# A second block that begins with the weights still in place, operand loads on GpSimd's queue, and pinned column sums

## The chip, the core and the metric

The kernel runs on one core of a Trainium2 chip. TensorE multiplies matrices, VectorE (DVE in the profile) and ScalarE (ACT) work on tiles, GpSimd (POOL) computes a few small values and issues some DMAs, and SyncE (SP) only issues DMAs. The metric is the device time of one execution in microseconds (us); lower is better. A difference of 0.2%, about 4.4 us here, is what a measurement of this kernel can tell from no change.

## What is computed

One encoder layer on a sequence of 2048 rows of 1024 columns: a normalisation and an input projection, windowed attention beside a state-space scan, a joint output projection ("the join" below), and then a gated feed-forward part and a last normalisation. The change touches the feed-forward part:

```
h = rms_norm(x, norm_ffn_g)                        # 2048 x 1024
up = depthwise_conv(h @ w_up, conv_w, conv_b)      # w_up: 1024 x 5632, conv of width 3 along the rows
gate, val = up[..., :2816], up[..., 2816:]
x = x + (silu(gate) * val) @ w_down                # w_down: 2816 x 1024
return rms_norm(x, norm_final_g)
```

All of it is float32. The kernel splits every operand into a high part in TensorE's rounded float32 format and a low rest, and adds three products (high by high, high by low, low by high).

## The kernel before

Both feed-forward products go by Strassen's scheme in Winograd's form: a step computes a 2 by 2 block product with seven half-size products instead of eight, from sums and differences of the quarter matrices. TensorE works through steps. The rows are cut into two blocks of 1024 (b = 0, 1), and block b has 22 steps, one for each pair f of a gate tile and a value tile of `w_up`. After these 44 steps (n = 0 to 43) come 24 steps of the down projection in three parts. A step of the up projection has 7 products of 12 matmuls, each matmul 128x128 by 128x512.

**Moving operand** (the rows of the block; seven matrices named in `BOP`: "11", "t2", "21", "t1", "t3", "t4", "22"). `put(b, m)` loads one of them from HBM in two halves of 512 KB through a ring of three buffers (tile `braw`, pool `fr`) and splits each half: ScalarE writes the high part (L1009), VectorE the low part (L1010). They stay for a whole block. The last step of a block calls `put` for the next block after each product. For block one, `ffn_open` loads the first four during the join, and `meet` the last three, after the last turn of the join. All these loads are issued by SyncE (L1007).

**Stationary operand** (the weights of one f). `up_raw` loads the gate tile and the value tile (`uraw`, L1015, 512 KB each). `stationary` splits g (L1048 on ScalarE, L1049 on VectorE), forms the sums s0 and s1 (tiles `st`) and splits s2, g2, s1 and s4 from them. There is one buffer of each split tile, so a split for the next step waits until the products that read the tile are over. In block one the sums are four VectorE operations of 128x512 (L1061 to L1064), and SyncE then stores both to HBM (L1072, L1073). In block two the two sums are loaded (L1058, L1059) instead.

**One step** on TensorE: products 1 and 6 of the step, 4 of the step before, 2, then 3 of the step before, 5 and 7. The PSUM results are joined on VectorE (L1159, L1164, L1175, L1179, L1180) and ScalarE (L1156 copies product 1 to `cu`, L1172); `up_conv` then does the convolution (L1232 to L1243), Silu (L1246) and the gate (L1247), and GpSimd stores the result (L1250).

**Sums of `w_down`.** For the down projection, `down_sums` makes 11 sets of sums: SyncE loads two rows of tiles into the same ring of three buffers (tile `bsum`, L1099), VectorE does four operations of 128x512 (L1101 to L1104), GpSimd stores four results (L1106). A table `SUMS` names the steps that call it: in block one the loads at n = 9, 12, 15, 18 and the operations one step after each, in block two every second step from n = 24.

A scheduler reorders each engine's instructions, so the place in the code is not the place in the queue. It drew the first eleven sums' operations forward: those of block one stand within its first four steps, those of block two within that block's first six steps. `keep_in_program_order` ties an instruction to its place in the program.

`rstd` (L124, L125) computes the scale of a row's normalisation: one VectorE operation and a power on GpSimd, needed by each turn of the join.

## Time and profile before

| | |
|---|---|
| time, median of 3 runs | 2192.28 us (2191.86 to 2192.76) |
| the profiled execution's own time | 2187.94 us |
| its span, first to last instruction | 2186.1 us |
| mean granted TensorE clock | 0.980 |
| TensorE busy | 2074.6 us (95%) |
| VectorE busy | 1692.2 us (77%) |
| ScalarE busy | 1047.1 us (48%) |
| GpSimd busy | 142.7 us (7%) |
| first product of step 0 (block one) | 852.77 us |
| first product of step 22 (block two) | 1284.24 us |

Busy time is a share of the whole span. How well a stage feeds TensorE is seen in the stretches: the number of matmuls that start in one, and the idle time ahead of an instruction with the engine that ended it.

### The profile page before, as it was taken

The page shows a single profiled execution, that of the slowest core. Times are in us where ns is not written, and L with a number is a line of the kernel's source. Part 1 is how long each engine was busy: PE and PEld are TensorE (multiplying, and loading weights), DVE is VectorE, ACT ScalarE, POOL GpSimd, SP SyncE. Part 2 cuts the span into 40 slices and gives each one's busy share as a digit, 9 for nine tenths or more (in the row PEclk, how much of TensorE's full clock was granted, in tenths as well). Part 3 has the DMA queues.
Part 4 walks back from the last instruction along what each step waited for, and adds up shares of the span by engine and source line. Part 5 has one row for each costly group of instructions (what it writes and reads, how often), then busy time and mean ns, then how long its engine had stood idle before and what let it go on. Part 6 is the DMA issues. An engine that isn't in the chain of part 4 may idle for free.

```text
span 2186.1 us, 28134 instructions
## 1 busy us (share of the span) xinstructions
PE 2074.6 (95%) x10000; PEld 1668.5 (76%) x10000; DVE 1692.2 (77%) x2977; ACT 1047.1 (48%) x1836; POOL 142.7 (7%) x230
## 2 busy tenths in 40 slices
PE   7998988799999998999999999999999999999997
PEld 5787777577777776788888877788888777787886
DVE  8978888675566557898888888877777987867875
ACT  5524444776666654444444464444444623324332
POOL 0400000000000000100000001100000000000111
PEclk9999999899999999999999999999999999999999
DMA  7965665523243229763334377743444667756542
GB/s 278 340 187 152 198 185 163 161 95 90 83 130 116 82 93 293 266 230 137 133 145 145 135 240 261 264 143 129 141 135 133 200 226 248 239 159 230 193 158 93
DMA packets 221612, 384.12 MB, mean 176 GB/s; under 512 B 15264, under 2 KB 136608, under 8 KB 221472
## 3 DMA queue, kind: packets, MB, share of 16 engines
q1 hardware_dynamic: 201744, 316.72, 45.5%
q0 software_dynamic: 16288, 62.92, 7.6%
q10 hardware_dynamic: 3440, 2.69, 0.4%
q8 instruction: 78, 1.28, 0.2%
q14 instruction: 62, 0.51, 0.1%
HBM read 254.88 MB, written 127.40 MB: 175 GB/s over the span
## 4 chain that ended last, share of the span: by engine, by line
PE 53%; issue 23%; DVE 10%; DMA 8%; ACT 3%; POOL 2%; SPq 1%; ACTq 0%; POOLq 0%; DVEq 0%
PE py L1132 13%; PE px L1132 8%; PE pz L1132 8%; PE po L78 3%; PE po L79 3%; PE po L80 3%; PE av L591 2%; PE ptp L581 2%; PE sp L558 2%; DMA kp_d<-kk 1%; PE pp L80 1%; PE pp L79 1%; PE pp L78 1%; PE gpt L669 1%; DMA m<-kp_d 1%
## 5 line engine op out<-in xcount | busy, mean ns | idle before, releaser
L1132 PE MATMUL px<-b,g1h 128*128 128x512 f32 x1056 | 328.0, 391 | 13.4 <-ACT cu L1156 13.4
L1132 PEld LDWEIGHTS px<-b,g1h 128*128 128x128 f32 x1056 | 199.4, 189 | 56.2 <-ACT cu L1156 14.6
L1132 PE MATMUL px<-b,g1l 128*128 128x512 f32 x528 | 206.8, 392 | 3.5 <-DVE g1l L1049 3.5
L1132 PE MATMUL py<-bt,g2h 128*128 128x512 f32 x528 | 168.9, 397 | 7.9 <-DVE cu L1179 7.9
L1132 PE MATMUL py<-bt,s2h 128*128 128x512 f32 x528 | 165.8, 395 | 10.1 <-ACT s2h L1048 10.1
L1132 PE MATMUL pz<-bt,s1h 128*128 128x512 f32 x528 | 163.7, 391 | 4.8 <-ACT s1h L1048 4.8
L1132 PE MATMUL pz<-b,s4h 128*128 128x512 f32 x528 | 162.8, 389 | 0.0
L1132 PE MATMUL py<-bt,s1h 128*128 128x512 f32 x528 | 162.6, 389 | 0.0
L1132 PEld LDWEIGHTS py<-bt,s2h 128*128 128x128 f32 x528 | 99.2, 189 | 33.6 <-ACT s2h L1048 13.7
L1132 PEld LDWEIGHTS py<-bt,g2h 128*128 128x128 f32 x528 | 100.8, 192 | 31.1 <-issue 5.4
L1132 PEld LDWEIGHTS px<-b,g1l 128*128 128x128 f32 x528 | 100.0, 189 | 25.3 <-DVE g1l L1049 4.4
L1132 PEld LDWEIGHTS pz<-bt,s1h 128*128 128x128 f32 x528 | 99.2, 188 | 26.3 <-ACT s1h L1048 5.9
L1132 PEld LDWEIGHTS pz<-b,s4h 128*128 128x128 f32 x528 | 99.1, 188 | 20.6
L1132 PEld LDWEIGHTS py<-bt,s1h 128*128 128x128 f32 x528 | 99.1, 188 | 20.6
L1048 ACT ACTIVATE g2h<-uraw 128x512 fp32r<-128x512 f32 x44 | 27.9, 634 | 176.7 <-PE py L1132 176.7
L1048 ACT ACTIVATE s1h<-st 128x1024 fp32r<-128x1024 f32 (+1 forms) x68 | 70.1, 1031 | 85.3 <-PE py L1132 78.0
L1132 PE MATMUL py<-bt,s2l 128*128 128x512 f32 x264 | 105.6, 400 | 3.1 <-DVE s2l L1049 3.1
L1164 DVE TENSOR_TENSOR cu<-py,cu 128x512 f32<-128x512 f32 x68 | 46.9, 690 | 74.6 <-PE py L1132 74.6
L1132 PE MATMUL py<-bt,g2l 128*128 128x512 f32 x264 | 104.4, 395 | 0.0
L1132 PE MATMUL pz<-bt,s1l 128*128 128x512 f32 x264 | 102.7, 389 | 0.0
L1132 PE MATMUL py<-bt,s1l 128*128 128x512 f32 x264 | 102.7, 389 | 0.0
L1132 PE MATMUL pz<-b,s4l 128*128 128x512 f32 x264 | 102.7, 389 | 0.0
(280 smaller groups left out, 5094.5 us busy)
## 6 DMA issues: line engine op xcount, KB each, us to landing
uraw<-in_w_up_dram SPq DMA_DIRECT2D x88, 512.0 KB
us<-st SPq DMA_DIRECT2D x44, 512.0 KB
st<-us SPq DMA_DIRECT2D x44, 512.0 KB
araw<-act SPq DMA_DIRECT2D x32, 512.0 KB
xr<-sum SPq DMA_DIRECT2D x32, 512.0 KB
xr<-in_xT_dram SPq DMA_DIRECT2D x30, 512.0 KB
act<-cv POOLq DMA_DIRECT2D x22, 512.5 KB, 3.1
bsum<-in_w_down_dram SPq DMA_DIRECT2D x22, 512.0 KB
```

What stands on the lines that cost most here:

```text
L78: nc.tensor.matmul(out, sh, mh, start=first and i == 0, stop=False)
L79: nc.tensor.matmul(out, sh, ml, start=False, stop=False)
L80: nc.tensor.matmul(out, sl, mh, start=False, stop=last and i == n - 1)
L558: nc.tensor.matmul(sp[:, :n], qTs[b][:, 4 * kv + j], kT[:, kv, i, slots], start=i == 0, stop=i == 1)
L581: nc.tensor.transpose(pt[:, 128 * j:128 * (j + 1)], sm[:, j, 128 * ki:128 * ki + 128], self.ident)
L591: nc.tensor.matmul(av[64 * o:64 * o + 64], vt[order[ki]][:, kv], ph4[:, o], start=ki == 0, stop=ki == len(order) - 1)
L669: nc.tensor.transpose(pt[:, 128 * k:128 * (k + 1)], src[:, 128 * k:128 * (k + 1)], self.ident)
L1048: S.activation(h[:, :c], src, AF.Copy)
L1132: nc.tensor.matmul(bank, x[:, k], o[:, y, k], start=first and k == 0 and i == 0, stop=k == kn - 1 and i == 2, skip_group_check=True)
L1164: V.tensor_tensor(old["vc"][:, lo], old["Y"], old["vc"][:, lo], op=ALU.add)
```

## The change

Five edits. (1) Block two goes through f = 21, 0, 1, ..., 20 instead of 0 to 21, and its first step (n = 22) takes the split weights that step 21 left in place; nothing is loaded or split for it. (2) The sums s0 and s1 are neither stored nor loaded: block two computes them with the same four VectorE operations as block one. (3) The 14 loads of the moving operand for block one are issued by GpSimd instead of SyncE. (4) The `put` calls for the last three moving operands of block one stand in step 0 behind the copy of product 1 (L1156 before) instead of in `meet`, ahead of it. (5) The four operations of `down_sums` are pinned to their places in the program. Line numbers of the changed kernel are lower by one around L1009, by five to eight from `stationary` on.

```diff
--- before.py
+++ after.py
@@ -105,7 +105,6 @@
         self.bop_d = [{m: d.tile([128, 4, HALF], F32, name=f"bo{b}{m}") for m in BOP} for b in (0, 1)]
         self.act_d = [d.tile([2 * n, 128, L], F32, name=f"act{c}") for c, n in enumerate(DN)]
         self.wsum_d = [{m: d.tile([128, n, HALF], F32, name=f"ws{c}{m}") for m in ("t1", "t2", "t3", "t4")} for c, n in enumerate(DN)]
-        self.usum_d = [d.tile([2, 128, 8, 128], F32, name=f"us{f}") for f in range(NF)]
         self.gN = None
         self.st_f = ExitStack()
         self.left = False
@@ -976,7 +975,7 @@
         self.operands(self.pool(st, "fb"), BOP[:2])
         self.pw = self.pool(st, "fu")
         yield
-        self.w0 = yield from self.up_weights(0, 0, self.pw)
+        self.w0 = yield from self.up_weights(0, self.pw)
         for n in BOP[:2]:
             yield from self.put(0, n)
         while not self.left:
@@ -1004,7 +1003,7 @@
                 r, c = int(n[0]) - 1, int(n[1]) - 1
                 f = DF[b - 2] + r * kn + k
                 src = self.a["w_down"][128 * f:128 * (f + m), HALF * c:HALF * (c + 1)].rearrange("(k p) c -> p k c", p=128)
-            nc.sync.dma_start(raw, src)
+            (nc.sync if b else nc.gpsimd).dma_start(raw, src)
             h = o[:, 0, k:k + m]
             nc.scalar.activation(h, raw, AF.Copy)
             nc.vector.tensor_tensor(o[:, 1, k:k + m], raw, h.bitcast(F32), op=ALU.subtract)
@@ -1031,13 +1030,9 @@
         self.sv = p.tile([128, 2 * NF, 2], F32, name="sv", bufs=1)
         pz = self.pool(st, "fpz", 2, space=PSUM)
         self.psq = self.pool(st, "fpq", space=PSUM)
-        for n in BOP[4:]:
-            for _ in self.put(0, n):
-                pass
         return p, pz
 
-    def stationary(self, g, v, n, pw, sums=None, keep=False):
-
+    def stationary(self, g, v, n, pw):
 
         nc = self.nc
         V, S = nc.vector, nc.scalar
@@ -1054,29 +1049,22 @@
         s0 = pw.tile([128, 8, 128], F32, tag="st0", name=self.nm("st0"))
         s1 = pw.tile([128, 8, 128], F32, tag="st1", name=self.nm("st1"))
         yield
-        if sums is not None and not keep:
-            nc.sync.dma_start(s1, sums[1])
-            nc.sync.dma_start(s0, sums[0])
-        else:
-            V.tensor_tensor(s0[:, lo], v[:, lo], v[:, hi], op=ALU.add)
-            V.tensor_tensor(s1[:, lo], s0[:, lo], g[:, lo], op=ALU.subtract)
-            V.tensor_tensor(s0[:, hi], g[:, lo], v[:, lo], op=ALU.subtract)
-            V.tensor_tensor(s1[:, hi], g[:, hi], s1[:, lo], op=ALU.subtract)
-            yield
+        V.tensor_tensor(s0[:, lo], v[:, lo], v[:, hi], op=ALU.add)
+        V.tensor_tensor(s1[:, lo], s0[:, lo], g[:, lo], op=ALU.subtract)
+        V.tensor_tensor(s0[:, hi], g[:, lo], v[:, lo], op=ALU.subtract)
+        V.tensor_tensor(s1[:, hi], g[:, hi], s1[:, lo], op=ALU.subtract)
+        yield
         s2, = split("s2", s1[:, lo], 4)
         a22, = split("g2", v[:, hi], 4)
         yield
         s1_, s3 = split("s1", s0[:, 0:2 * n], 8)
         s4, = split("s4", s1[:, hi], 4)
-        if keep:
-            nc.sync.dma_start(sums[1], s1)
-            nc.sync.dma_start(sums[0], s0)
         yield
         return {1: (a11, "11"), 2: (a12, "21"), 3: (s4, "22"), 4: (a22, "t4"), 5: (s1_, "t1"), 6: (s2, "t2"), 7: (s3, "t3")}
 
-    def up_weights(self, b, f, pw):
+    def up_weights(self, f, pw):
         g, v = (self.up_raw(f, i) for i in (0, 1))
-        return (yield from self.stationary(g, v, 4, pw, self.usum_d[f], b == 0))
+        return (yield from self.stationary(g, v, 4, pw))
 
     def down_rows(self, c, t, pw):
 
@@ -1098,10 +1086,10 @@
             for t, f in ((A, f0 + k), (B, f0 + n + k)):
                 nc.sync.dma_start(t.rearrange("p n c -> p (n c)"), self.a["w_down"][128 * f:128 * (f + 1), :])
             yield
-            V.tensor_tensor(C[:, 0], A[:, 1], A[:, 0], op=ALU.subtract)
-            V.tensor_tensor(C[:, 1], B[:, 1], A[:, 1], op=ALU.subtract)
-            V.tensor_tensor(A[:, 0], C[:, 1], A[:, 0], op=ALU.add)
-            V.tensor_tensor(B[:, 0], B[:, 0], A[:, 0], op=ALU.subtract)
+
+            for o, x, y, op in ((C[:, 0], A[:, 1], A[:, 0], ALU.subtract), (C[:, 1], B[:, 1], A[:, 1], ALU.subtract),
+                                (A[:, 0], C[:, 1], A[:, 0], ALU.add), (B[:, 0], B[:, 0], A[:, 0], ALU.subtract)):
+                self.tc.keep_in_program_order(V.tensor_tensor(o, x, y, op=op))
             for m, t in (("t1", C[:, 0]), ("t3", C[:, 1]), ("t2", A[:, 0]), ("t4", B[:, 0])):
                 nc.gpsimd.dma_start(self.wsum_d[c][m][:, k], t)
             yield
@@ -1113,7 +1101,8 @@
         V, S = nc.vector, nc.scalar
         lo, hi = slice(0, HALF), slice(HALF, BLK)
 
-        todo = [(b, f, f == NF - 1) for b in (0, 1) for f in range(NF)]
+
+        todo = [(0, f, f == NF - 1) for f in range(NF)] + [(1, (f - 1) % NF, f == NF - 1) for f in range(NF)]
         todo += [(2 + c, t, t == NB - 2) for c in range(3) for t in range(0, NB, 2)]
 
         def run(steps):
@@ -1140,7 +1129,10 @@
             if at:
                 b, f, _ = at
                 down = b >= 2
-                w = self.w0 if n == 0 else run(self.down_rows(b - 2, f, self.pw) if down else self.up_weights(b, f, self.pw))
+                if n == 0:
+                    w = self.w0
+                elif n != NF:
+                    w = run(self.down_rows(b - 2, f, self.pw) if down else self.up_weights(f, self.pw))
                 X, Y = (ps.tile([128, HALF], F32, tag=t, name=self.nm(t)) for t in ("px", "py"))
                 cur = {"w": w, "at": at, "Y": Y}
                 if n == 0:
@@ -1157,6 +1149,9 @@
                 if n:
                     product(cur, 6, Y, True)
                 V.tensor_tensor(gc[:, hi], Y, vc[:, hi], op=ALU.add)
+                if n == 0:
+                    for m in BOP[4:]:
+                        run(self.put(0, m))
                 if down:
                     V.tensor_tensor(gc[:, hi], gc[:, hi], xg[:, hi], op=ALU.add)
             if old:
```

ScalarE's queue at the end of the join, before: `hT` is the join's last turn, `bt_1888`, `bt_1889` and `b_1890` are "t3", "t4" and "22", and `cu_9050` is the copy of product 1 of step 0.

```order
L739 ACTIVATE hT_8986<-gpt_8981 128x512
L750 ACTIVATE hT_8996<-gpt_8990 128x512
L1009 ACTIVATE bt_1888_9011<-braw_9024 128x1024
L1009 ACTIVATE bt_1888_9011<-braw_9028 128x1024
L1009 ACTIVATE bt_1889_9012<-braw_9032 128x1024
L1156 ACTIVATE cu_9050<-px_8952 128x512
L1009 ACTIVATE bt_1889_9012<-braw_9036 128x1024
L1048 ACTIVATE g1h_9096<-uraw_9092 128x1024
L1009 ACTIVATE b_1890_9013<-braw_9040 128x1024
L1009 ACTIVATE b_1890_9013<-braw_9044 128x1024
```

ScalarE's queue at the same place, after:

```order
L738 ACTIVATE hT_8962<-gpt_8957 128x512
L749 ACTIVATE hT_8972<-gpt_8966 128x512
L1148 ACTIVATE cu_9002<-px_8928 128x512
L1008 ACTIVATE bt_1888_8987<-braw_9005 128x1024
L1008 ACTIVATE bt_1888_8987<-braw_9009 128x1024
L1008 ACTIVATE bt_1889_8988<-braw_9013 128x1024
L1043 ACTIVATE g1h_9072<-uraw_9068 128x1024
L1167 ACTIVATE cg_9001<-px_8928 128x512
L1043 ACTIVATE s1h_9090<-st_1904_9076 128x1024
L1008 ACTIVATE bt_1889_8988<-braw_9017 128x1024
```

The copy of product 1 (`cu`) moves from behind three splits of "t3" and "t4" to ahead of all of them.

GpSimd's queue there, after; the rows at L124 are the power operations of the join's normalisations, and before only these stood there:

```order
L1006 DMA braw_8848<-bo_112 128x1024
L124 TENSOR_TENSOR r_1820_8637<-rsv_8638,mhalf 128x1
L1006 DMA braw_8871<-bo_112 128x1024
L124 TENSOR_TENSOR ra_8667<-rsv_8668,mhalf 128x1
L1006 DMA braw_8895<-bo0t_113 128x1024
L124 TENSOR_TENSOR r_1860_8805<-rsv_8806,mhalf 128x1
L1006 DMA braw_8905<-bo0t_113 128x1024
L1006 DMA braw_9005<-bo0t_114 128x1024
L1006 DMA braw_9009<-bo0t_114 128x1024
L1006 DMA braw_9013<-bo0t_115 128x1024
L124 TENSOR_TENSOR r_1879_8920<-rsv_8921,mhalf 128x1
L1006 DMA braw_9017<-bo0t_115 128x1024
L1006 DMA braw_9021<-bo_116 128x1024
L1006 DMA braw_9025<-bo_116 128x1024
```

The loads of "21" (`bo_112`), "t1" (`bo0t_113`), "t3" (`bo0t_114`), "t4" (`bo0t_115`) and "22" (`bo_116`) now stand between the powers, and `r_1879`, the one of the join's last turn, has three loads of "t3" and "t4" ahead of it.

SyncE's queue before, where the loads of "t1", "t3" and "t4" stood between the stores and loads of the join's last turns (L731, L735):

```order
L1007 DMA braw_8929<-bo0t_113 128x1024
L731 DMA bo1t_122<-hq_8883 512x1x128
L802 DMA x_d<-x_1863_8838 128x1024
L1007 DMA braw_9024<-bo0t_114 128x1024
L735 DMA hq_8978<-bo_117 128x4x128
L735 DMA hq_8978<-bo_119 128x4x128
L731 DMA bo1t_121<-hx_8942 512x1x128
L1007 DMA braw_9028<-bo0t_114 128x1024
L731 DMA bo1t_120<-hx_8942 512x1x128
L731 DMA bo_123<-hT_8996 512x1x128
L731 DMA bo1t_118<-hq_8978 512x1x128
L731 DMA bo1t_122<-hq_8978 512x1x128
L1007 DMA braw_9032<-bo0t_115 128x1024
```

These loads are gone from SyncE's queue; the order of the others there is as it was.

VectorE's queue early in block two, before; `bsum` are the sums of `w_down`:

```order
L1241 SCALAR_TENSOR_TENSOR cv_12422<-cg_12176,cw,cv_12422 128x1023
L1242 SCALAR_TENSOR_TENSOR cv_12422<-sv,cw,cv_12422 128x2
L1101 TENSOR_TENSOR bsum_12869<-bsum_12867 128x512
L1243 SCALAR_TENSOR_TENSOR cv_12422<-cg_12176,cw,cv_12422 128x1024
L1179 TENSOR_TENSOR cu_12330<-py_12327,cu_12330 128x512
L1049 TENSOR_TENSOR s2l_12450<-st_2414_12446,s2h_12449 128x512
L1180 TENSOR_TENSOR cu_12330<-pz_12328,cu_12330 128x512
L1247 TENSOR_TENSOR cv_12428<-cv_12422,cv_12428 128x1025
L1049 TENSOR_TENSOR s1l_12458<-st_2413_12445,s1h_12457 128x1024
L1102 TENSOR_TENSOR bsum_12869<-bsum_12868,bsum_12867 128x512
```

VectorE's queue in a step of block two that has sums, after (L1092 is `down_sums`, L1052 and L1054 are sums of the next weights):

```order
L1242 TENSOR_TENSOR cv_12918<-cv_12912,cv_12918 128x1025
L1092 TENSOR_TENSOR bsum_12783<-bsum_12781 128x512
L1092 TENSOR_TENSOR bsum_12783<-bsum_12782,bsum_12781 128x512
L1052 TENSOR_TENSOR st_2513_13089<-uraw_13083 128x512
L1092 TENSOR_TENSOR bsum_12781<-bsum_12783,bsum_12781 128x512
L1151 TENSOR_TENSOR cg_12968<-py_12966,cu_12969 128x512
L1092 TENSOR_TENSOR bsum_12782<-bsum_12782,bsum_12781 128x512
L1054 TENSOR_TENSOR st_2513_13089<-uraw_13081,uraw_13083 128x512
L1159 TENSOR_TENSOR cu_12820<-py_12817,cu_12820 128x512
L1044 TENSOR_TENSOR g2l_12954<-uraw_12937,g2h_12953 128x512
L1236 SCALAR_TENSOR_TENSOR cv_13067<-cu_12820,cw,cv_13067 128x1023
L1237 SCALAR_TENSOR_TENSOR cv_13067<-sv,cw,cv_13067 128x2
```

The four operations on `bsum` stand together at the end of a step, behind the gate's product (L1242), and no more in the middle of the convolution, ahead of the low part of s2 (L1049 s2l before).

## Rows read from the trace of the kernel before

**Rows 1.** the head of the page: span, and busy time of TensorE and VectorE
```profile
span 2186.1 us, 28134 instructions
...
PE 2074.6 (95%) x10000; PEld 1668.5 (76%) x10000; DVE 1692.2 (77%) x2977; ACT 1047.1 (48%) x1836; POOL 142.7 (7%) x230
```

**Rows 2.** windows: stretch, length, each engine's busy time (instructions), clock, DMA
```profile
870.00:880.00 10.00, 1.43 (x3) 1.16 (x4) 3.80 (x4) 2.60 (x3) 0.00 (x0) 0.60 1.00 324
880.00:890.00 10.00, 10.00 (x41) 8.15 (x40) 7.03 (x8) 6.05 (x7) 0.00 (x0) 0.89 0.91 311
900.00:960.00 60.00, 59.12 (x261) 48.62 (x260) 56.53 (x73) 27.31 (x40) 9.22 (x17) 1.00 0.76 269
1000.00:1250.00 250.00, 250.00 (x1104) 207.02 (x1103) 209.59 (x250) 113.95 (x159) 7.05 (x13) 1.00 0.38 139
1280.00:1320.00 40.00, 35.16 (x142) 28.12 (x141) 36.51 (x39) 24.54 (x33) 2.46 (x5) 0.91 0.72 238
1340.00:1420.00 80.00, 72.89 (x310) 58.52 (x309) 64.49 (x86) 34.94 (x47) 13.09 (x25) 0.98 0.77 280
1440.00:1690.00 250.00, 250.00 (x1088) 203.37 (x1089) 180.29 (x220) 115.71 (x154) 6.41 (x12) 1.00 0.42 137
1720.00:1760.00 40.00, 34.31 (x147) 26.79 (x146) 39.53 (x58) 20.69 (x29) 2.13 (x4) 1.00 0.71 234
```

**Rows 3.** TensorE's timeline at the first feed-forward step (start, length, line, names, idle before)
```profile
878.57 1.22 PE L1132 MATMUL px<-b,g1h 128*128 128x512 f32 x2 [11.56 <-ACT cu L1156]
...
883.14 0.62 PE L1132 MATMUL py<-bt,s1h 128*128 128x512 f32 x2
...
888.59 0.61 PE L1132 MATMUL py<-bt,g2h 128*128 128x512 f32 x2
```

**Rows 4.** ScalarE's timeline in the same stretch
```profile
867.95 0.60 ACT L750 ACTIVATE hT<-gpt 128x512 f32<-128x512 f32 x1 [3.47 <-DVE hx L743]
...
876.97 1.06 ACT L1009 ACTIVATE bt<-braw 128x1024 fp32r<-128x1024 f32 x1 [5.38 <-DMA braw<-bo0t]
877.93 0.58 ACT L1156 ACTIVATE cu<-px 128x512 f32<-128x512 f32 x1
881.42 1.06 ACT L1009 ACTIVATE bt<-braw 128x1024 fp32r<-128x1024 f32 x1 [2.91 <-DMA braw<-bo0t]
```

**Rows 5.** SyncE's DMA issues there, GpSimd's one operation, one split on VectorE
```profile
830.20 1.18 SPq L1007 DMA_DIRECT2D braw<-bo0t  x2
...
844.82 0.33 SPq L1007 DMA_DIRECT2D braw<-bo  x1
...
860.48 0.55 POOL L125 TENSOR_TENSOR r<-rsv,mhalf 128x1 f32<-128x1 f32 x1 [11.15 <-DVE rsv L124]
...
864.03 1.22 DVE L1010 TENSOR_TENSOR bt<-braw,bt 128x1024 fp32r<-128x1024 f32 x1 [1.68 <-ACT bt L1009]
```

**Rows 6.** ScalarE, then TensorE, in block two's first step
```profile
1287.16 1.06 ACT L1009 ACTIVATE bt<-braw 128x1024 fp32r<-128x1024 f32 x1 [0.56 <-DMA braw<-bo1t]
1288.12 1.04 ACT L1048 ACTIVATE s1h<-st 128x1024 fp32r<-128x1024 f32 x1
...
1289.22 1.22 PE L1132 MATMUL pz<-bt,s1h 128*128 128x512 f32 x2 [4.37 <-ACT s1h L1048]
```

**Rows 7.** VectorE and TensorE early in block two
```profile
1346.21 0.69 DVE L1101 TENSOR_TENSOR bsum<-bsum 128x512 f32<-128x512 f32 x1 [3.38 <-DMA bsum<-in_w_down_dram]
1346.82 1.28 DVE L1243 SCALAR_TENSOR_TENSOR cv<-cu,cw,cv 128x1024 f32<-128x1024 f32 x1
...
1355.05 0.73 PE L1132 MATMUL py<-bt,s2h 128*128 128x512 f32 x2 [2.48 <-ACT s2h L1048]
```

**Rows 8.** VectorE's groups in 1440 to 1690 (count, busy, mean ns, idle before)
```profile
L1241 DVE SCALAR_TENSOR_TENSOR cv<-cg,cw,cv 128x1023 f32<-128x1023 f32 x13 | 16.7, 1286 | 9.3 <-ACT cv L1239 9.3
```

**Rows 9.** TensorE at the turn to the down projection
```profile
1751.03 0.50 PE L1132 MATMUL px<-b,g1l 128*128 128x512 f32 x1 [3.27 <-DVE g1l L1049]
```

## The prediction

> **What bounds the kernel now.** I read the head of the page first: TensorE is busy 2074.6 of 2186.1 us [rows 1], so a gain can only come from the stretches where it waits. The view of windows finds them. Where nothing waits, in 1000 to 1250, 1104 matmuls start in 250 us [rows 2]; a matmul then takes 250/1103 = 0.2267 us (one is counted more, since a stretch cuts one at its edge), and a step of 84 takes 19.04 us. Any stretch can be held against that pace: its length over 0.2267, plus one, is what should start in it; what is missing, times 0.2267, is its loss [rows 2]:
> - 1280 to 1320, block two's first step: 177.5 due, 142 there, 8.0 us lost.
> - 1340 to 1420, early in block two: 354 due, 310 there, 10.0 us.
> - 1440 to 1690, the rest of block two: 1104 due, 1088 there, 3.6 us.
> - 900 to 960, early in block one: 266 due, 261 there, 1.1 us.
> - 1720 to 1760, the turn to the down projection: 177.5 due, 147 there, 6.9 us.
>
> At the start of the feed-forward part matmuls of the join run among the others, so I read that place from TensorE's timeline: it stands idle for 11.56 us until 878.57, for `cu` [rows 3]. Last, the timelines of the engine waited for say why, and the order of the queues says whether the change touches that.
>
> **Step 0: copy of product 1 ahead of the splits, loads on GpSimd.** ScalarE copies `cu` at 877.93, behind a split at 876.97 that waited 5.38 us for a load [rows 4]. Now the copy follows the last `hT` of the join directly. That ran at 867.95 for 0.60 us [rows 4], so `cu` is done near 869.1, and product 2 runs from there to 871.8 at full pace. Before it took 883.14 - 878.57 = 4.57 us instead of 2.72 [rows 3], while the granted clock was 0.60 and 0.89 of full [rows 2], which is partly the 1.2 GHz level, after 11.56 us of rest. The rest is now some 2 us. Product 7 needs "t3", whose halves ScalarE and VectorE split right behind the copy, in 1.06 and 1.22 us a half [rows 4, 5], by about 872.5; at 2.72 us a product it ends near 874.6, product 1 of step 1 near 877.3, and then product 4 of step 0 can start, which started at 888.59 [rows 3]. That is 11.3 us earlier, the upper bound. It asks that "t4" is there. Its last half was split on ScalarE at 881.42 to 882.48 [rows 4], and on VectorE until about 883.7. If its load lands as it did, product 4 starts at worst at 883.7 instead of 888.59, 4.9 us earlier: the lower bound. SyncE issued a load of "t1" at 830.20 and the next one, of "21", only at 844.82 [rows 5], because its queue holds the join's stores between them; GpSimd has none of these, so "21" and "t1" come earlier, and the ring's buffers come free earlier for "t3" and "t4". But all DMA engines are busy in this stretch (share 1.00 in 870 to 880) [rows 2], so I take 7.5 us, nearer to the lower bound.
>
> The Trainium skill speaks against the second half of this: "Trainium Kernel Development and Optimization", Key Constraints, says that DMAs issued by SyncE, ScalarE and GpSimd share 16 DMA engines, and that issuing from several of them saves only the sequencers' issue time. By that alone the loads would land when they did, and this term would be 4.9 us. The share of 1.00 is in accord with it; the 14.6 us between two issues on SyncE are a queue's waiting, which the sentence does not cover.
>
> What can be lost here: a power of the join's normalisation now stands behind loads that wait for a free buffer. The last ran at 860.48 [rows 5], and three loads of "t3" and "t4" are ahead of it. The third needs the buffer of the second "t1" half. If "t1" comes early, that half is split by about 858 and nothing is late; if it comes as before, the split of 864.03 frees the buffer at 865.25 [rows 5], and the last turn slips by some 5 us. Net of this the term lies between 0 and 11.3 us.
>
> **Block two's first step.** TensorE waited 4.37 us until 1289.22 for s1 of the new weights, whose ScalarE half stood behind splits of `bt` that waited for loads [rows 6]. With the weights of step 21 there is nothing to load or split before this step. The moving operands are renewed as before. At best all 8.0 us come back. But VectorE still has 14 low parts to make there, and it works 36.51 of the 40 us [rows 2]; the weights of n = 23 are then made in a full queue, and I charge one wait of 2 us and half as much again for the clock. I take 5 us, with ends 0 and 8.
>
> **Early block two.** VectorE stands still at the head of its queue for `bsum`, 3.38 us at 1346.21, the split s2 comes after that, and TensorE waits 2.48 us until 1355.05 [rows 7]. The same pattern returns in each of these steps. Now the four operations come one step behind their loads, so they should find their data, and s2 no longer waits for stored sums from HBM either. Of 10.0 us I take 9, and 5 if half of the waits had another cause. The 1.1 us early in block one go too, since its sums now lie in later steps with more room.
>
> **Four more operations in each of 21 steps.** One of 128x512 takes 0.69 us, and the next instruction starts 0.61 us after it [rows 7], so 2.4 us a step and 51 us in all: VectorE must have them hidden. In 1440 to 1690 it is busy 180.29 us in 12.9 steps (of 19.04 x 1104/1088 = 19.32 us), 13.95 a step; with the sums 16.35 of 19.04. In block one, with the same four operations and nearly the same order, it is busy 209.59 us in 13.1 steps, 15.96 a step, and TensorE runs at full pace [rows 2]. This is the best evidence that they fit. On seven steps (n = 25 to 37) `down_sums` adds 2.4: 18.75 of 19.04, followed by a step of 16.35, on average 17.55. In 900 to 960 VectorE is busy 56.53 of 60 us and TensorE loses only 1.1 us in three steps [rows 2]. So I charge 0.2 us for each of the seven, 1.5 in all, and keep 0 and 7 as ends. In return the steady loss of 3.6 us goes: there s2 was split late, behind the gate's operations, and it now has block one's place. The stores of the sums in block one (22 x 1 MB, DMA share 0.38) [rows 2] hid nothing and win nothing.
>
> **The turn to the down projection.** VectorE is busy 39.53 of 40 us there [rows 2], and TensorE waits 3.27 us for it [rows 9]. The order hardly changes; the last weights of block two add 2.4 us of sums a step ahead of it. I take 0, between -3 and +2.
>
> **Sum.** 7.5 + 5 + 9 + 1.1 + 3.6 - 1.5 + 0 = 24.7 us. The profiled execution took 2187.94 us, so 2163.2; the median of the runs shown is 4.3 us above it (2192.28), so 2167.6, say 2168 us.
>
> **Rivals.**
> 1. GpSimd's queue holds up the join: the power of the last turn waits for a buffer. For it: three loads ahead of it, DMA share 1.00. Against: between 830.20 and 844.82 SyncE's queue, not the ring, kept "21" back [rows 5]. Then step 0 gives 7.5 - 5 = 2.5 us, the sum is 19.7, the time 2172.6; with two turns held, 2178.
> 2. The waits in block two move rather than go: with `bsum` away the next thing that s2 needs is late, because the sums themselves are now computed in front of it. For it: s2 now needs two results of VectorE more. Against: it needs them in block one too, at full pace [rows 2]. Then early block two gives 3, the first step 2, the steady part 0 and the charge stays: 7.5 + 2 + 3 + 1.1 - 1.5 = 12.1 us, or 2180.2.
> 3. The other side: VectorE becomes the bound of block two. It idles 69.7 us in 1440 to 1690, 5.4 a step, of it 9.3 us in 13 instructions for one ScalarE result alone [rows 8]. If this idle time is not filled by the sums, a step takes 16.35 + idle. Break-even: the other terms are worth 7.5 + 5 + 9 = 21.5 us, 1.0 us for each of 21 steps, so it decides from 19.04 + 1.0 - 16.35 = 3.7 us of idle a step. With 4.5, between block one's 3.1 and 5.4, a step takes 20.85, the block loses 38 us, and the time is 2192.3 - 21.5 + 38 = 2209. Against it: in block one the idle time shrank to 3.1 us without any loss [rows 2].
> 4. Nothing: the early waits return as waits for DMA, and rivals 1 and 2 come together, within 4.4 us of before.
>
> **How the numbers follow.** The forecast with its neighbours (2158 to 2174) has 0.62, rival 1 0.13, rival 2 0.14, rival 4 0.05, rival 3 0.06. The best ends of all terms give 11.3 + 8 + 10 + 1.1 + 3.6 + 2 = 36, or 2156. The range goes from there to 2184, past rivals 1 and 2. A change of under 0.2% (4.4 us) cannot be told from none; faster by more than that has 0.62 + 0.13 + 0.14 = 0.89, the same 0.05, slower 0.06.
>
> **What would show it.** Right: TensorE's idle time ahead of product 2 of step 0 falls from 11.56 to about 2 us; 1280 to 1320 and 1340 to 1420 show at least 164 and 350 matmuls; 1440 to 1690 shows 1100 or more, with VectorE busy some 215 us; VectorE waits for no `bsum`. Wrong: the last `hT` of the join is later than 868; a wait for s2, g1 or s1 returns in every second step of block two (the steps with sums); or POOL's powers wait behind loads.

## The result and the profile after

The changed kernel takes 2166.53 us in the median of 4 runs (2165.11 to 2167.66), the kernel before 2192.52 us (4 runs): a ratio of 0.988, 95% interval 0.9863 to 0.9897, so 26 us faster. The prediction was 2168 us in a range of 2156 to 2184. The profiled execution took 2167.66 us, 20.3 us less than the profiled one before; the rest of the 26 us is that the one before lay 4.6 us under its median and this one 1.1 us above.

The head of the page after, which answers to [rows 1]:

```profile
span 2165.9 us, 28012 instructions
...
PE 2067.8 (95%) x10000; PEld 1668.7 (77%) x10000; DVE 1734.0 (80%) x3056; ACT 1047.1 (48%) x1831; POOL 151.2 (7%) x244
```
And the view of windows after (a window is a stretch of the execution), which answers to [rows 2], with 1320 to 1440 added for the experiments below (stretch, length, busy us and instructions of TensorE, weight load, VectorE, ScalarE and GpSimd, then clock, DMA share, GB/s):

```profile
870.00:880.00 10.00, 9.46 (x38) 7.36 (x37) 5.08 (x7) 5.48 (x7) 0.20 (x1) 0.86 0.65 185
900.00:960.00 60.00, 58.09 (x255) 47.48 (x254) 52.41 (x64) 29.20 (x41) 1.64 (x3) 1.00 0.26 84
1280.00:1320.00 40.00, 38.29 (x168) 31.10 (x168) 37.17 (x42) 24.06 (x31) 1.08 (x2) 1.00 0.50 168
1320.00:1440.00 120.00, 120.00 (x531) 99.34 (x530) 108.21 (x144) 58.08 (x76) 7.56 (x14) 1.00 0.34 119
1340.00:1420.00 80.00, 80.00 (x355) 66.24 (x354) 72.88 (x99) 38.82 (x50) 6.49 (x12) 1.00 0.40 138
1440.00:1690.00 250.00, 250.00 (x1105) 207.01 (x1104) 223.93 (x297) 122.91 (x161) 18.36 (x34) 1.00 0.36 124
1720.00:1760.00 40.00, 36.24 (x151) 28.80 (x150) 36.26 (x55) 12.09 (x19) 2.65 (x5) 0.96 0.71 231
```

In 1280 to 1320, 168 matmuls start where 142 did; in 1340 to 1420 it is 355 (all that fit) instead of 310, in 1440 to 1690 1105 instead of 1088. VectorE is busy 223.93 us in that last stretch, against 180.29, and TensorE loses nothing. At the turn to the down projection little moved (151 and 147). The one place that disappoints is the start, where 900 to 960 now holds 255 matmuls, and 261 before.

A finer measure than a fixed stretch is the start of product 3 of each step, read from TensorE's timeline. The first line counts from an instruction of ScalarE that both kernels have in the join, before and after:

```profile
817.12 0.60 ACT L739 ACTIVATE hT<-gpt 128x512 f32<-128x512 f32 x1 [0.58 <-PE gpt L669]
```

And after:

```profile
817.32 0.60 ACT L738 ACTIVATE hT<-gpt 128x512 f32<-128x512 f32 x1 [0.58 <-PE gpt L668]
```

From there the lengths are, in us:

| | before | after | gained | predicted |
|---|---|---|---|---|
| from this hT to product 3 of step 1 | 96.0 | 95.1 | 0.9 | 7.5 |
| to that of step 3 | 39.3 | 38.1 | 1.2 | 1.1 |
| from step 20 to 22, the turn of the blocks | 46.6 | 40.3 | 6.3 | 5 |
| to step 27 | 105.6 | 95.2 | 10.4 | 9 |
| to step 40 | 251.1 | 247.5 | 3.6 | 3.6 - 1.5 |
| to the end | 506.8 | 508.7 | -1.9 | 0 |

The steps between (3 to 20) take 19.04 us each in both. The lines sum to 20.5 us; the span is 20.3 us shorter, and 0.2 us lies ahead of `hT`. The first and the last line are no larger than what executions differ by: in four more profiles of kernels that are alike up to there (`changed_again`, `natural_order`, `sums_unpinned`, `sums_twice`) the first length is 93.6 to 96.2 us, which makes the gain -0.2 to 2.3 us; the last one is 506.6 to 512.0 us in the profiles below, `sums_twice` left out.

### The profile page after: what moved, and what is told of

It reads as the page before. It is cut to its first block, busy times and chain, and to the rows that moved or that the text cites. A ratio compares the mean times of both kernels' runs of the same rounds, so it can differ in the third digit from the quotient of the medians.

```text
span 2165.9 us, 28012 instructions
## 1 busy us (share of the span) xinstructions
PE 2067.8 (95%) x10000; PEld 1668.7 (77%) x10000; DVE 1734.0 (80%) x3056; ACT 1047.1 (48%) x1831; POOL 151.2 (7%) x244
## 4 chain that ended last, share of the span: by engine, by line
PE 73%; DMA 11%; DVE 10%; ACT 3%; issue 2%; SPq 0%; POOL 0%; ACTq 0%; POOLq 0%; DVEq 0%
PE py L1121 21%; PE pz L1121 14%; PE px L1121 14%; PE po L78 3%; PE av L590 3%; DMA kp_d<-kk 2%; PE po L79 2%; PE po L80 2%; PE sp L557 2%; PE ptp L580 2%; PE pp L80 1%; PE pp L79 1%; PE pp L78 1%; PE gpt L668 1%; DMA m<-kp_d 1%
## 5 line engine op out<-in xcount | busy, mean ns | idle before, releaser
L1121 PE MATMUL py<-bt,g2h 128*128 128x512 f32 x528 | 164.4, 392 | 9.8 <-DVE cu L1174 9.8
L1043 ACT ACTIVATE s1h<-st 128x1024 fp32r<-128x1024 f32 (+1 forms) x67 | 69.4, 1036 | 127.0 <-PE py L1121 119.6
L1121 PEld LDWEIGHTS pz<-b,s4h 128*128 128x128 f32 x528 | 99.1, 188 | 20.5
## 6 DMA issues: line engine op xcount, KB each, us to landing
uraw<-in_w_up_dram SPq DMA_DIRECT2D x86, 512.0 KB
araw<-act SPq DMA_DIRECT2D x32, 512.0 KB
xr<-sum SPq DMA_DIRECT2D x32, 512.0 KB
xr<-in_xT_dram SPq DMA_DIRECT2D x30, 512.0 KB
bsum<-in_w_down_dram SPq DMA_DIRECT2D x22, 512.0 KB
xn<-in_x_dram SPq DMA_DIRECT2D x16, 512.0 KB
```

The costliest lines, as they stand in the source:

```text
L1043: S.activation(h[:, :c], src, AF.Copy)
L1121: nc.tensor.matmul(bank, x[:, k], o[:, y, k], start=first and k == 0 and i == 0, stop=k == kn - 1 and i == 2, skip_group_check=True)
```

## The experiments

Every kernel is the changed one with one edit, unless it says otherwise. Each was profiled once. The stages ahead are the same in all of them, yet the `hT` at 817.12 above ran between 815.93 and 821.53: executions differ by 5 us before the change comes in. So places are compared by their distance from that instruction, and medians where they differ by more. The experiments were measured on different chips, each beside the kernel before (whose medians there are 2188.9 to 2193.5 us); across experiments the ratio to it therefore says more than the difference of two medians.

**1. All loads on SyncE** (`loads_sync`)

```
-            (nc.sync if b else nc.gpsimd).dma_start(raw, src)
+            nc.sync.dma_start(raw, src)
```

> The changed kernel, with all 14 loads for block one issued by SyncE again. In the changed kernel the join's last hT ran at 875.06 us instead of 867.95 before, which took back most of step 0's gain. Theory S (order): with the loads on GpSimd, the scheduler put two splits on VectorE, and two loads on GpSimd, ahead of the join's own rsv and power, so hx of the turn before last began at 833.97 instead of 830.55; with SyncE they stand behind it again, so hx is back within 1 us of 830.6, the last hT within 2 us of 868, and product 4 of step 0 starts near 882 to 884, since t4 comes as late as before; time 2161 to 2165. Theory D (DMA share): the loads, being early, took bandwidth from the join's stores; this too brings the join back, so these two are told apart by loads_scalar. Rival Q: the loads on GpSimd were worth their cost, since t3 and t4 land earlier; then step 1 starts later than in the changed kernel and the time is 2168 to 2172.

Measured: 2164.17 us (2160.69 to 2166.8), 0.9868 of before (0.9842 to 0.9894). First the changed kernel at the join: VectorE's, GpSimd's and ScalarE's timelines (start, length, engine, line, names, idle before).

```profile
830.18 1.22 DVE L1009 TENSOR_TENSOR b<-braw,b 128x1024 fp32r<-128x1024 f32 x1
831.31 0.14 DVE L123 TENSOR_SCALAR rsv<-ossq 128x1 f32<-128x1 f32 x1
...
832.83 1.22 DVE L1009 TENSOR_TENSOR bt<-braw,bt 128x1024 fp32r<-128x1024 f32 x1 [0.77 <-ACT bt L1008]
833.97 1.28 DVE L808 SCALAR_TENSOR_TENSOR hx<-x,r,gfr 128x1024 f32<-128x1024 f32 x1
...
831.92 0.53 POOL L1006 DMA_DIRECT2D braw<-bo  x1 [1.73 <-DVE rsv L123]
832.46 0.57 POOL L124 TENSOR_TENSOR r<-rsv,mhalf 128x1 f32<-128x1 f32 x1
...
875.06 0.60 ACT L749 ACTIVATE hT<-gpt 128x512 f32<-128x512 f32 x1 [3.76 <-DVE hx L742]
...
876.03 2.96 ACT L1008 ACTIVATE bt<-braw 128x1024 fp32r<-128x1024 f32 x3
...
884.05 1.06 ACT L1008 ACTIVATE bt<-braw 128x1024 fp32r<-128x1024 f32 x1 [0.83 <-DMA braw<-bo0t]
```

The power at 832.46 is behind a load; its operand `rsv` at 831.31 is behind a split that began at 830.18, and `hx` at 833.97 is behind a split at 832.83. With the loads on SyncE:

```profile
830.67 1.28 DVE L808 SCALAR_TENSOR_TENSOR hx<-x,r,gfr 128x1024 f32<-128x1024 f32 x1
...
869.49 0.60 ACT L749 ACTIVATE hT<-gpt 128x512 f32<-128x512 f32 x1 [1.67 <-DVE hx L742]
...
879.29 1.06 ACT L1008 ACTIVATE bt<-braw 128x1024 fp32r<-128x1024 f32 x1 [4.65 <-DMA braw<-bo0t]
...
882.62 1.05 ACT L1008 ACTIVATE bt<-braw 128x1024 fp32r<-128x1024 f32 x1
```

`hx` is back at 830.67, and the last `hT` at 869.49 instead of 875.06. But "t4" is late again, its halves at 879.29, after 4.65 us of waiting for the load, and 882.62, and product 4 of step 0 starts here (TensorE's timeline):

```profile
886.60 0.62 PE L1121 MATMUL py<-bt,g2h 128*128 128x512 f32 x2
```
In the changed kernel it starts at:

```profile
885.40 0.62 PE L1121 MATMUL py<-bt,g2h 128*128 128x512 f32 x2
```

From the `hT` near 817 that is 69.4 and 68.1 us (before 71.5 [rows 3]). So the join came back, as theories S and D both said, and the time lies in their range. But product 4 did not start at 882 to 884. Rival Q was right that three of the four halves of "t3" and "t4" land later than from GpSimd's queue, and wrong on the time (2168 to 2172). On GpSimd's queue "t3" and half of "t4" lay ready when the late copy came (three splits without a pause at 876.03), but the last half of "t4" had to wait for a buffer that those splits free, and came at 884.05. In sum GpSimd's queue was worth nothing that these runs can show.

**2. The first eight loads on SyncE, the last six on GpSimd** (`loads_split`)

```
-            (nc.sync if b else nc.gpsimd).dma_start(raw, src)
+            (nc.sync if b or n in BOP[:4] else nc.gpsimd).dma_start(raw, src)
```

> The changed kernel, with the first eight loads (11, t2, 21, t1) on SyncE as before and the last six (t3, t4, 22) on GpSimd. Theory S: the join is as with all loads on SyncE (last hT near 868), and t4 lands some us earlier than there, so product 4 of step 0 starts near 878 to 882: 2160 to 2164, 0 to 3 us less than loads_sync. Theory D: loads of t3 and t4 that are early compete with the join's last stores; the last hT is 2 us or more later than in loads_sync and the time 2164 to 2168.

Measured: 2162.39 us (2160.97 to 2165.89), 0.9867 (0.9846 to 0.9888). Its last `hT` ran at 869.30, as in `loads_sync` and as theory S said (by theory D it is 2 us or more later), and product 4 of step 0 started here:

```profile
881.50 0.62 PE L1121 MATMUL py<-bt,g2h 128*128 128x512 f32 x2
```

That is 64.1 us from the `hT` near 817 instead of 71.5: 7.4 us, about what the prediction had put down. Whether that stays was asked by a second pair.

> The kernel of loads_split once more, beside the changed kernel on the same chip. If its 7.4 us at the first product 4 are real, it is faster than the changed kernel by 3 to 6 us: 2160 to 2164 where the changed kernel has 2165 to 2168. Rival: the difference of the medians (2162.4 and 2166.5) came from different chips and the start of the execution, and the two are within 1 us.

> The changed kernel itself, beside split_again on the same chip: 2165 to 2168.

Measured on one chip: 2167.57 us (2159.62 to 2172.19) and 2168.16 us (2165.61 to 2169.34). The intervals of their ratios (0.9866 to 0.9905, 0.9877 to 0.9906) lie on each other, so the rival is right: the two are within 1 us. In this execution of the split version the join was late for another reason (ScalarE's timeline, then TensorE's):

```profile
873.75 0.60 ACT L749 ACTIVATE hT<-gpt 128x512 f32<-128x512 f32 x1 [8.31 <-DVE hx L742]
...
874.89 1.22 PE L1121 MATMUL px<-b,g1h 128*128 128x512 f32 x2 [6.94 <-ACT cu L1148]
```

The last `hT` waited 8.31 us for VectorE's `hx`, which itself waited 6.32 us for the load of `hq`, and TensorE 6.94 us for `cu`. Product 4 started 68.2 us from the first `hT`. So the split can win some us at step 0, but in this pair of executions the join's own transfers took as much back, and no version is shown to beat the changed kernel.

**3. The first eight loads on ScalarE's queue** (`loads_scalar`)

```
-            (nc.sync if b else nc.gpsimd).dma_start(raw, src)
+            (nc.sync if b or n not in BOP[:4] else nc.scalar).dma_start(raw, src)
```

> The changed kernel, with the first eight loads on ScalarE's queue and the last six on SyncE. The loads are nearly as early as on GpSimd, but on VectorE only one split stands ahead of the rsv of the turn before last, as before the change, and no load stands ahead of a power on GpSimd. Theory S: hx of that turn begins within 1 us of 830.6. Theory D: it is as late as in the changed kernel, 833 or later, whatever the order. Time: 2162 to 2167 by S (ScalarE's own queue now holds loads that wait for a buffer), 2166 to 2170 by D.

Measured: 2166.57 us (2164.96 to 2168.32). VectorE's timeline at the turn before last:

```profile
831.67 1.22 DVE L1009 TENSOR_TENSOR b<-braw,b 128x1024 fp32r<-128x1024 f32 x1
832.80 0.15 DVE L123 TENSOR_SCALAR rsv<-ossq 128x1 f32<-128x1 f32 x1
...
834.05 1.28 DVE L808 SCALAR_TENSOR_TENSOR hx<-x,r,gfr 128x1024 f32<-128x1024 f32 x1 [0.44 <-POOL r L124]
```

Read from the shared `hT` (819.28 here), `hx` of that turn begins after 14.8 us: before it was 13.4, in the changed kernel 16.7. Counted from the shared `hT` this is 1.3 us later than before and 1.9 earlier than in the changed kernel, so neither theory has the number (within 1 us by S, as late as the changed kernel by D). What holds it is seen: one split ahead of `rsv`. That speaks for order more than for the DMA share, but the loads here were also a few us later than on GpSimd, so theory D is not excluded for the remainder. That the queue of these first eight loads decides is clear from all profiles together: `hx` begins after 13.4 us in each of the five profiles with these loads on SyncE, and after 16.2 to 17.3 us in each of the eight with them on GpSimd.

**4. The last three operands in `meet` again** (`puts_in_meet`)

```
-                if n == 0:
-                    for m in BOP[4:]:
-                        run(self.put(0, m))
+        for n in BOP[4:]:            # in meet, as before
+            for _ in self.put(0, n):
+                pass
```

> The changed kernel, with the put calls of t3, t4 and 22 in meet again, ahead of the copy of product 1. The prediction's mechanism: ScalarE's copy stands behind splits that wait for loads again, TensorE idles 8 us or more before product 2 of step 0, and the kernel loses 3 to 8 us: 2169 to 2175. Rival: with the loads earlier on GpSimd's queue the splits find their data, the copy is not held, and the time is that of the changed kernel within 2 us.

Measured: 2175.45 us (2171.84 to 2177.06), 0.9922 (0.99 to 0.9943): 9 us slower than the changed kernel, by the medians and by the ratios. ScalarE's timeline, then TensorE's:

```profile
876.88 2.94 ACT L1008 ACTIVATE bt<-braw 128x1024 fp32r<-128x1024 f32 x3
879.72 0.59 ACT L1151 ACTIVATE cu<-px 128x512 f32<-128x512 f32 x1
...
885.56 1.06 ACT L1008 ACTIVATE bt<-braw 128x1024 fp32r<-128x1024 f32 x1 [5.26 <-DMA braw<-bo0t]
...
880.36 0.94 PE L1124 MATMUL px<-b,g1h 128*128 128x512 f32 x2 [2.46 <-ACT cu L1151]
...
894.66 0.63 PE L1124 MATMUL py<-bt,g2h 128*128 128x512 f32 x2
```

The copy `cu` stands behind three splits again. They found their data, so TensorE idled only 2.46 us, not 8: in this the mechanism named ahead was wrong, and the rival right. The loss comes a little later. The fourth split waits 5.26 us for its load, the weights of step 1 (`g1h`) stand behind it on ScalarE, and TensorE waits 1.72 us for them; product 4 starts 75.6 us after the first `hT` (819.09 here), where the five profiles of kernels that are alike up to there, the changed one among them, have 67.5 to 70.0. So this edit is worth 6 to 8 us at product 4, given that the loads are on GpSimd.

**5. Block two in natural order** (`natural_order`)

```
...                                  # parts of two lines
-  [(1, (f - 1) % NF, f == NF - 1) for f in range(NF)]
+  [(1, f, f == NF - 1) for f in range(NF)]
-                elif n != NF:
+                else:
```

> The changed kernel, with block two in the order f = 0 to 21, so that its first step loads and splits its own weights. Theory: the wait at the turn of the blocks returns; the two steps around it, which lose 2.2 us in the changed kernel and 8.5 before, lose 6 to 10, and the rest of block two stays at 19.04 us a step; time 2170 to 2174. Rival: the changed kernel gains there because SyncE no longer loads stored sums, so that the moving operands land earlier; then the two steps lose 4 us or less and the time stays within 2 us of the changed kernel's 2166.5.

Measured: 2172.33 us (2167.15 to 2174.66), 0.9919 (0.9893 to 0.9945). From step 20 to 23 the turn loses 5.7 us (2.2 in the changed kernel), a little under the range given, and the rest of block two keeps its pace. In the same steps the kernel before loses 8.3, so of 6.1 us gained there the reuse is 3.5; the other 2.6 come with the other edits together (pinning alone gives 1.1: 7.2 us are lost in `before_pinned`, below).

**6. Pinned or not, computed or stored** (`sums_unpinned`, `sums_stored`, `stored_unpinned`, `before_pinned`)

```
-                self.tc.keep_in_program_order(V.tensor_tensor(o, x, y, op=op))
+                V.tensor_tensor(o, x, y, op=op)         # sums_unpinned, stored_unpinned
-        V.tensor_tensor(s0[:, lo], ...)                 # and the other three
+        if sums is not None and not keep:               # sums_stored, stored_unpinned
+            nc.sync.dma_start(s1, sums[1])
+            nc.sync.dma_start(s0, sums[0])
...
```

> The changed kernel, with the four operations of down_sums left to the scheduler. Theory P: the stalls early in block two came from these operations, drawn forward to the head of VectorE's queue before their loads landed; they return, the steps from n = 23 to 28 lose 6 to 10 us again, and the time is 2172 to 2178. Rival L: the stalls came from the stored sums that s2 waited for; these are gone here too, so the steps keep 19.04 us and the time stays within 2 us of 2166.5.

> The changed kernel, with s0 and s1 stored in block one and loaded in block two again (for f = 0 to 20), and 84 VectorE operations less. Rival L: early block two loses 4 us or more of its 10.4 again, and the 0.27 us a step of the late s2 returns, 3 to 5 us: 2172 to 2180. Theory P: early block two keeps its full pace, since the pinned operations find their data; only the late s2 can return, 0 to 5 us: 2166 to 2172. If VectorE's added work had cost time that I don't see, the kernel would get faster than 2164.

> The changed kernel with both undone: sums s0 and s1 stored and loaded, and the operations of down_sums left to the scheduler. Unpinning alone cost 3.3 us in n = 23 to 30, storing alone none beyond 0.3 us a step. Theory J (joint): an early operation only stalls VectorE for long when its loads stand in line behind those of the stored sums, so both together bring back 8 to 11 us in n = 23 to 28, and 0.27 us a step after that; 2180 to 2186. Rival (each its own): the losses add to about 3.3 + 1.5 in those steps, and the time is 2179 to 2182.

And in the kernel before, `down_sums` pinned and nothing else:

> The kernel before, with the four operations of down_sums pinned and nothing else changed. Theory J (joint): the stalls of n = 23 to 28 need the early operations as well as the stored sums' loads; pinned, those steps lose 3 us or less instead of 10.4, the 0.3 us a step and the wait at the turn of the blocks (8.5 us) stay, and so does step 0's wait of 11.6 us: 2181 to 2185. Rival (each its own): pinning is worth only what unpinning cost in the changed kernel, 3.3 us: 2188 to 2190.

Measured, by the windows 1320 to 1440 (530 matmuls fit) and 1440 to 1690 (1104 fit). Not pinned (`sums_unpinned`):

```profile
1320.00:1440.00 120.00, 118.34 (x521) 97.12 (x520) 111.56 (x153) 54.92 (x74) 15.11 (x28) 1.00 0.54 185
1440.00:1690.00 250.00, 249.50 (x1101) 206.25 (x1100) 215.30 (x281) 122.17 (x161) 8.55 (x16) 1.00 0.26 90
```

Stored and loaded (`sums_stored`):

```profile
1320.00:1440.00 120.00, 119.31 (x519) 96.57 (x518) 92.12 (x114) 57.03 (x77) 7.56 (x14) 1.00 0.50 170
1440.00:1690.00 250.00, 249.82 (x1088) 203.20 (x1087) 192.50 (x241) 116.86 (x156) 17.83 (x33) 1.00 0.53 179
```

Both (`stored_unpinned`):

```profile
1320.00:1440.00 120.00, 105.99 (x450) 85.09 (x449) 91.66 (x120) 49.09 (x67) 15.64 (x29) 0.97 0.70 240
1440.00:1690.00 250.00, 249.96 (x1088) 202.81 (x1087) 181.04 (x220) 116.19 (x155) 6.92 (x13) 1.00 0.41 136
```

The kernel before, then the same pinned (`before_pinned`):

```profile
1320.00:1440.00 120.00, 112.86 (x484) 91.01 (x482) 97.12 (x127) 53.30 (x71) 17.04 (x32) 0.99 0.71 251
...
1320.00:1440.00 120.00, 119.93 (x525) 97.75 (x524) 91.51 (x115) 56.44 (x75) 7.56 (x14) 1.00 0.52 173
```

| loss in 1320 to 1440 (time, ratio to before) | pinned | not pinned |
|---|---|---|
| sums computed | 0 us (2166.53, 0.988) | 2.1 us (2171.92, 0.9921) |
| sums stored and loaded | 2.6 us (2177.72, 0.9951) | 18.2 us (2191.42, 1.0001) |

Neither theory of a single cause holds: theory P named 6 to 10 us for the first, rival L 4 us or more for the second. The losses don't add: 2.1 and 2.6 alone, 18.2 together (the missing matmuls times 0.2267 us), more than the 8 to 11 that theory J had named, and the time is above its 2180 to 2186. With both undone the kernel is as slow as before (1.0001, 0.9988 to 1.0014), though all else of the change is in it. And pinning alone makes the old kernel 0.9939 of its time (0.9919 to 0.9959, 2179.95 us) and takes the loss there from 10.5 us (484 matmuls) to 1.2. Theory J holds in kind: the big loss needs both causes. Its sizes were off, and why the two together cost 18.2 us in `stored_unpinned` and 10.5 in the kernel before was not taken apart. How one makes the other worse is seen on VectorE's timeline of `stored_unpinned`, and behind it on ScalarE's and TensorE's:

```profile
1360.08 2.15 DVE L1100 TENSOR_TENSOR bsum<-bsum,bsum 128x512 f32<-128x512 f32 x3 [3.07 <-DMA bsum<-in_w_down_dram]
...
1372.66 0.69 DVE L1100 TENSOR_TENSOR bsum<-bsum,bsum 128x512 f32<-128x512 f32 x1 [2.25 <-DMA bsum<-in_w_down_dram]
...
1376.57 1.06 ACT L1249 ACTIVATE cv<-cv 128x1025 f32<-128x1025 f32 x1 [5.01 <-DVE cv L1246]
1377.53 0.61 ACT L1044 ACTIVATE s2h<-st 128x512 fp32r<-128x512 f32 x1
...
1378.20 1.22 PE L1129 MATMUL py<-bt,s2h 128*128 128x512 f32 x2 [4.80 <-ACT s2h L1044]
```

An operation drawn forward waits 2.25 and 3.07 us at the head of VectorE's queue for a load. The convolution behind it is late, the Silu waits 5.01 us for that on ScalarE, the split of `s2h` stands behind the Silu, and TensorE waits 4.80 us. From 1310 to 1440 VectorE waits 7.4 us for loads of `bsum` here and 0.7 us in `sums_unpinned`. The stored sums are 1 MB a step more to load, at a DMA share of 0.70 against 0.54 with computed sums. That the `bsum` loads land later for this reason is argued from it and was not measured by itself. Not all of the loss takes this path: a wait of 3.24 us of TensorE, at 1422.35, is for an `s2h` that waited 3.02 us for the stored sums themselves. 1440 to 1690 shows the other cost of stored sums, 1088 matmuls whether pinned or not: the late s2, 0.3 us a step. `sums_stored` is 11 us slower than the changed kernel by the medians and 16 by the ratios; its profiled execution is 9.4 us longer. These two stretches explain 6 of them; 3.2 lie ahead of the shared `hT` and 1.8 between it and product 3 of step 1 (96.9 us), where executions differ; about 2 are made up in other places, and what the ratios show beyond the profile was not found.

**7. Four more operations in each step of block two** (`sums_twice`; the same sum again, into the same place)

```
+        for _ in range(extra):        # 4 in block two
+            V.tensor_tensor(s0[:, lo], v[:, lo], v[:, hi], op=ALU.add)
         V.tensor_tensor(s0[:, lo], v[:, lo], v[:, hi], op=ALU.add)
```

> The changed kernel, with the first of the four sums computed five times in each of the 21 steps of block two: 4 operations, 2.4 us of VectorE a step more, the same result. By the prediction's own figures VectorE then has 18.75 us of work in a plain step and 21.15 in one with sums of w_down, against 19.04 for TensorE. The pairs from n = 25 to 37 should take 39.9 us or more instead of 38.08, so 12 us or more are lost there in all, and a plain step 19.1 to 19.5. If VectorE were not near its limit, nothing would change.

Measured: 2183.39 us, one run; its `hT` ran 4.2 us later than in the changed kernel, which leaves 11.5 us of its span. From step 20 to 40 it loses 7.5 us, where 12 or more were expected; 4.8 lie behind step 40, where executions differ by as much. Windows in the steps with sums of `w_down`, and after the last of them:

```profile
1460.00:1500.00 40.00, 39.38 (x171) 31.26 (x169) 39.41 (x56) 18.19 (x25) 3.25 (x6) 1.00 0.36 132
1640.00:1680.00 40.00, 40.00 (x178) 33.02 (x177) 39.74 (x55) 18.51 (x26) 1.15 (x3) 1.00 0.25 80
```

The last five pairs with sums take 39.5 us, a little less than expected, plain steps 19.05 to 19.16. In 1640 to 1680 VectorE is busy 39.74 of 40 us and TensorE starts its full 178 matmuls.

## Why the prediction was right, point by point

**What bounds the kernel.** Right: what was read as missing matmuls in each stretch of block two came back (168, 355 and 1105 where 164, 350 and 1100 were named). The loss of the turn to the down projection, 6.9 us, was counted too and stays, as forecast.

**Step 0: wrong by size, and two of its steps failed.** The term was 7.5 us, forecast for the start of product 4. There it measured 3.4 (71.5 to 68.1 us), between its ends of 0 and 11.3, and 0.9 at product 3 of step 1.

The first step that failed is "`cu` is done near 869.1", because `hT` did not stay at 867.95: it ran at 875.06. A last `hT` later than 868 had been named as a sign of being wrong, and for this term it was one. The sign of TensorE's wait ahead of product 2, which fell from 11.56 us [rows 3] to 0.44, came true and yet is not the gain: TensorE reaches that place later, since it now waits 3.36 us for `s2h` at 865.36, which stands behind the late join on ScalarE. With the copy behind the splits again (experiment 4) the wait is 2.46 us, so the copy's place is worth 2 of those 11 us there. Rival 1 had the right place and the wrong instruction. It looked at the last power and the three loads ahead of it; that power ran at 865.13, right behind its `rsv` at 864.82. But 3.2 of the 6.9 us (both from the `hT` near 817) were lost at `hx` of the turn before, and less in GpSimd's queue than in VectorE's, where the scheduler, seeing the operands sooner, set two splits ahead of the join's own work; the rest grew in the last turn and was not taken apart. The order was there to be read, and the working looked only at the copy's engine and at GpSimd.

The second is the reading that SyncE's queue, not the ring, kept "21" back. The load of "21" at 844.82 [rows 5] needs the buffer of the second half of "11", and in the kernel before VectorE's split frees that only here:

```profile
843.58 1.22 DVE L1010 TENSOR_TENSOR b<-braw,b 128x1024 fp32r<-128x1024 f32 x1
```

It ends at 844.80; the last store ahead of the load had left at 844.20. So the ring was the last to hold it. (The loads at 830.20 are of "t2", not of "t1".) In the changed kernel that split runs at 830.18 and the load at 831.92; with the loads on SyncE again they are back at 843.71 and 844.95. The earlier load and the earlier split go together, and it is this split that `rsv` waits behind. And the last half of "t4" got nothing from GpSimd's queue: its load waited 13.80 us there for a buffer, went out at 879.80 instead of 873.10, and its split began at 884.05 instead of 881.42, so that the bound of 4.9 us, by which it lands as before, failed as well.

From product 4 of step 0 to product 3 of step 1 another 2.5 us went, most of them where VectorE, with its queue still full, made s2 late for product 6 of step 2 (TensorE's timeline, then VectorE's):

```profile
902.86 0.73 PE L1121 MATMUL py<-bt,g2h 128*128 128x512 f32 x2 [0.48 <-DVE cu L1174]
...
905.25 0.50 PE L1121 MATMUL py<-bt,s2l 128*128 128x512 f32 x1 [1.42 <-DVE s2l L1044]
...
904.51 0.68 DVE L1044 TENSOR_TENSOR s2l<-st,s2h 128x512 fp32r<-128x512 f32 x1
```

The Trainium skill ("Trainium Kernel Development and Optimization", Key Constraints), by which another issuing engine saves only issue time, was nearer in its result (4.9 us) than the 7.5: GpSimd or SyncE makes no difference here (68.1 and 69.4 us). The runs don't show it as the reason, since three of the four halves of "t3" and "t4" did land earlier (by 4.7, 3.6 and 6.5 us); the gain was paid back in the join.

**Turn of the blocks: right, 6.3 for 5.** What is left is the wait foreseen, on s2 in a full VectorE queue; it measured 1.71 us (TensorE's timeline):

```profile
1308.23 0.50 PE L1121 MATMUL py<-bt,s2l 128*128 128x512 f32 x1 [1.71 <-DVE s2l L1044]
```

**Early block two: right in size, 10.4 for 9, and half right in cause.** VectorE does not wait for `bsum` any more. But the term gave pinning and computing their parts as if each had its own; experiment 6 shows that either alone removes most of it. In the kernel before, pinning alone takes the length from step 22 to 27 from 105.6 to 96.2 us; the whole change takes it to 95.2.

**Four operations more: right that they fit.** The charge of 1.5 us for steps with sums measured 0. VectorE's 223.93 us in 1440 to 1690 are 9 more than the "some 215" named as a sign: that number left out the sums of `w_down`, of which 20 operations, 12 us, now run in this stretch. Rival 3 (idle time that can't be filled) is refuted by experiment 7: in plain steps VectorE's idle time shrank to under 1% before TensorE lost anything.

**Turn to the down projection: right.** The same wait, 3.26 us for 3.27 [rows 9]. On TensorE's timeline after:

```profile
1729.37 0.74 PE L1121 MATMUL px<-b,g1l 128*128 128x512 f32 x1 [3.26 <-DVE g1l L1044]
```

Behind it 1.9 us were lost, most of them in the down projection, which no edit touches and which differs by more from one execution to the next.

**The sum: met partly by luck.** Step 0 gave 6.6 us less and the end 1.9, the other terms 4.3 more, and 0.2 us lies ahead of `hT`, so the profiled execution gained 20.3 us where 24.7 were forecast. That the time came out 1.5 us under the forecast all the same is because the median was put 4.3 us above the profiled execution, as before, and came out 1.1 us below it.

## What to carry to other kernels

Count the instructions that start in each stretch against the pace of a full one: it gives what every stall costs without a theory, and in the four stretches whose cause the change removed the gain came within 2 us of it. What it does not give is which stalls a change will remove. An operation that waits at the head of an in-order queue costs what the load's queue makes it wait, so here pinning it and unloading that queue were mostly one gain, not two. When operands are made to arrive sooner, look where a scheduler now puts the work on them: ahead of the chain that was to be helped, it can take back all that the earlier load brought.

## What the runs showed of the hardware

VectorE ran at 39.74 of 40 us of work beside a TensorE at full pace (`sums_twice`), and its sums of 128x512 took 0.68 to 0.69 us there, as in the changed kernel. Executions of kernels that are alike up to there reached the same `hT` between 815.93 and 821.53 us, a spread larger than most terms of this change.
